# Expert 0 loaded before the router has run, the overflow branch behind the second pass, and two modulation vectors summed on VectorE

## The chip, the cores and the metric

The kernel runs as one program on one core of a Trainium2 chip. The metric is device time in microseconds (us) from one launch. The engines are TensorE (PE, with its weight loads as PEld), VectorE (DVE), ScalarE (ACT), GpSimd (POOL) and SyncE (SP), whose queue issues the loads of weights from HBM.

## The reference

`x` is 256 tokens of 1024 numbers. Two blocks follow one another, each of two layers. The first block is an even layer and an odd layer, and each layer has a token mixer and a mixture of 16 experts:

```python
mod = cond @ mod_w[layer] + mod_b[layer]            # six vectors of 1024 per layer
h = rms_norm(x, mix_norm_g[layer]) * (1 + sc1) + sh1
x = x + g1 * (even_mixer or odd_mixer)(h)
h = rms_norm(x, ffn_norm_g[layer]) * (1 + sc2) + sh2
x = x + g2 * moe(h)                                 # two of 16 experts per token
# moe, for the tokens of expert e:  (silu(xb @ w1[e]) * (xb @ w3[e])) @ w2[e]
# odd_mixer: proj = h @ od_in; conv of width 4; sigmoid gates; linear recurrence over
#            the tokens; gelu(y) * state; @ od_out
```

The second block has attention of three kinds and a dense MLP in each of its two layers, with six modulation vectors per layer for the tokens and for a context. All numbers are float32, and the six weights of an expert (two halves each of w1, w3 and w2) are 1 MB each, 96 MB per layer.

## The kernel before

The program goes through its stages once, in this order: even mixer and its output projection (to 181 us), router of layer 0 (to 217), experts of layer 0 (to 466), odd mixer and its output projection (to 582), router of layer 1 (to 620), experts of layer 1 (to 866), second block (to the end).

**Weights.** `weights` opens a pool for a stage with a ring of `raw` tiles: "long" has 11 tiles of 0.5 MB (the mixers), "wide" 9 tiles of 1 MB (router and experts), "short" 6 of 0.5 MB (second block). `load` (L321) takes the next tile and issues one DMA on SP's queue. That queue is in order: a load whose tile is still read holds up what stands behind it. In the mixers `linear` splits each weight into a high part on ScalarE (L332, `wh`) and a low part on VectorE (L325, `wl`) and multiplies three times on TensorE (L344 to L346). The experts' weights go to TensorE in float32 as they are (L959).

**Modulation vectors.** Each vector is a sum over eight loads of 0.5 MB. `mod_steps` makes eight units of it, which wait in a list and which `fill`, `need` and `settle` take off between other work. A unit is by default matmuls on TensorE into a bank of PSUM (L406); where `onv` holds an entry, VectorE multiplies and adds the load into tiles instead (L391 for the first load, L393 for the others), and TensorE only adds up the partitions at the end. Before, only vectors of the second block are summed on VectorE, with two conditions each.

**Experts.** `router` ranks the 16 experts by their number of tokens; `idi` holds the numbers in order of rank, and SP reads a register from it (L889) before it can address the weights. `PASSES` groups ranks: a pass of one rank has 128 columns of tokens, a pass of two has 64 per expert, and a pass of four 32 per expert, with the experts side by side in TensorE's array. `prep` gathers the tokens of a pass (L925 on VectorE, L933 to L944 on TensorE), `up_` multiplies by w1 and w3 (into `psab`), `down` by w2 (into `psY`), `combine` adds the results to `xT` (L1000). `sources` lists the loads in the order of use, and `taken` issues a load when its turn in the program comes and a tile is free. At the last pass but one (`p == NP - 2`) all engines come to a branch (L804): if an expert has more tokens than its columns, a loop serves the rest. With the inputs at hand the loop is not entered.

**Odd mixer.** Two loops over eight blocks of `od_in` (L1060 and L1062 apply the convolution on VectorE; L1087 copies the second half of the projection), with one modulation unit behind each block. Between the loops lie the gates and the recurrence: sigmoids, tanh, exponentials and logarithms on ScalarE (L293), two multiplications per block on GpSimd (L1072, L1081), a subtraction (L1079) and a scan (L1082) on VectorE.

A scheduler places the instructions of a stage on each engine within the order of the code; what stands where is read from the built programs below.

## Time and profile before

| | us |
|---|---|
| median of 3 runs (lowest, highest) | 1956.85 (1954.48, 1958.96) |
| the profiled execution | 1955.22 |
| its span in the trace | 1953.4 |
| experts of layer 0, 217 to 466 | 249 |
| odd mixer and output projection, 466 to 582 | 116 |
| experts of layer 1, 620 to 866 | 246 |
| second block, 866 to 1953.4 | 1087.4 |

The profile page has one line per 40 equal slices of the span (48.8 us each) for the engines, the granted clock of TensorE (PEclk) and the DMA engines, each digit a share in tenths; tables of busy time by window and by line; and lists of waits. A wait is named by who waited and who ended it.

### The profile page before, as it was taken

To read this page: it belongs to the slowest core of one execution; us is meant where nothing else is said; L and a number is where in the kernel's file an instruction comes from. 1 tells how busy PE (TensorE), PEld (TensorE's weight loads), DVE (VectorE), ACT (ScalarE), POOL (GpSimd) and SP (SyncE) were. 2 spreads that over 40 slices of the span, in tenths; PEclk is the share of its full clock that TensorE was granted. 3 is DMA by queue.
4 is the path that set the end of the run, shared out by engine and by line. 5 is a ranking of instruction groups with operands and counts; after the bars stand their busy time and mean duration, and the time that the engine had idled before them with its cause. 6 is when DMAs were issued, how large, how long until landed. Compare 5 with 4: busy or idle time off the path is not lost. (4 is left out here: it accounts for less than half of the span.)

```text
span 1953.4 us, 29087 instructions
## 1 busy us (share of the span) xinstructions
PE 1758.2 (90%) x11198; PEld 1256.4 (64%) x11198; DVE 1078.6 (55%) x2298; ACT 741.2 (38%) x1461; POOL 70.7 (4%) x88
## 2 busy tenths in 40 slices
PE   5999689967897799689999999999999999989997
PEld 4866234414783344237655779888888786669996
DVE  4987212104654112048778367678855767666665
ACT  3556100003642000124767355232323656544443
POOL 0000000000200000000010001000000200010000
PEclk8999899978998999889999999999999999989999
DMA  9685999997649999984100675555543220245551
GB/s 378 242 285 193 382 413 419 371 381 311 242 164 369 417 423 380 386 343 156 35 21 33 218 253 188 176 172 187 188 129 130 97 93 22 76 153 182 183 184 44
DMA packets 94361, 440.46 MB, mean 225 GB/s; under 512 B 10240, under 2 KB 10368, under 8 KB 69376
## 3 DMA queue, kind: packets, MB, share of 16 engines
q1 hardware_dynamic: 94208, 438.44, 60.0%
q8 instruction: 93, 1.52, 0.3%
q14 instruction: 60, 0.49, 0.1%
HBM read 437.35 MB, written 1.05 MB: 224 GB/s over the span
## 5 line engine op out<-in xcount | busy, mean ns | idle before, releaser
L332 ACT CAST wh<-raw 128x1024 fp32r<-128x1024 f32 (+1 forms) x258 | 261.4, 1016 | 281.8 <-PE psL L346 209.8
L325 DVE TENSOR_TENSOR wl<-raw,wh 128x1024 fp32r<-128x1024 f32 (+1 forms) x258 | 305.3, 1185 | 97.8 <-ACT wh L332 97.4
L959 PE MATMUL psab<-raw,xg 128*32 128x512 f32 (+2 forms) x1024 | 226.2, 705 | 76.1 <-DMA raw<-w 62.8
L344 PE MATMUL psL<-h,wh 128*128 128x256 f32 (+1 forms) x800 | 258.4, 323 | 7.6 <-ACT h L340 7.6
L345 PE MATMUL psL<-h,wl 128*128 128x256 f32 (+1 forms) x800 | 257.8, 323 | 4.0 <-DVE wl L325 3.9
L346 PE MATMUL psL<-h,wh 128*128 128x256 f32 (+1 forms) x800 | 256.4, 321 | 0.0
L959 PEld LDWEIGHTS psab<-raw,xg 128*32 128x32 f32 (+2 forms) x1024 | 73.9, 147 | 221.7 <-issue 193.7
L344 PE MATMUL psL<-gh,wh 128*128 128x256 f32 (+1 forms) x576 | 185.1, 322 | 0.0
L345 PE MATMUL psL<-gh,wl 128*128 128x256 f32 (+1 forms) x576 | 184.6, 321 | 0.0
L344 PEld LDWEIGHTS psL<-h,wh 128*128 128x128 f32 x800 | 154.2, 193 | 23.4 <-ACT h L340 8.3
L973 DVE SCALAR_TENSOR_TENSOR sa<-sa,gs,psab 128x512 f32<-128x512 f32 x14 | 10.5, 747 | 282.5 <-PE psab L959 282.5
L345 PEld LDWEIGHTS psL<-h,wl 128*128 128x128 f32 x800 | 154.2, 193 | 18.5 <-DVE wl L325 5.1
L346 PEld LDWEIGHTS psL<-h,wh 128*128 128x128 f32 x800 | 153.9, 193 | 14.2 <-issue 4.2
L959 PE MATMUL psY<-raw,at 128*32 128x512 f32 (+2 forms) x512 | 113.1, 611 | 9.3 <-DMA raw<-w 8.4
L346 PE MATMUL psL<-o,wh 128*128 128x256 f32 (+1 forms) x384 | 119.3, 311 | 0.3
L344 PEld LDWEIGHTS psL<-gh,wh 128*128 128x128 f32 x576 | 109.5, 190 | 14.5 <-issue 5.8
L345 PEld LDWEIGHTS psL<-gh,wl 128*128 128x128 f32 x576 | 109.5, 190 | 11.1 <-issue 3.7
L340 ACT CAST yh<-psY 128x512 fp32r<-128x512 f32 x28 | 16.4, 586 | 245.5 <-PE psY L959 245.5
L346 PE MATMUL psL<-gl,wh 128*128 128x256 f32 (+1 forms) x288 | 91.9, 319 | 0.0
L1525 ACT ACTIVATE t<-psL 128x256 f32<-128x256 f32 (+1 forms) x72 | 32.8, 456 | 139.1 <-PE psL L346 139.1
L1123 DVE SCALAR_TENSOR_TENSOR xT<-psL,mod2T,xT 128x256 f32<-128x256 f32 x80 | 38.6, 483 | 84.2 <-PE psL L346 84.0
L344 PE MATMUL psL<-hh,wh 128*128 128x256 f32 x256 | 77.8, 305 | 7.0 <-ACT hh L518 5.5
(449 smaller groups left out, 3340.9 us busy)
## 6 DMA issues: line engine op xcount, KB each, us to landing
raw<-w SPq DMA_DIRECT2D x192, 1024.0 KB, 11.7
raw<-fc SPq DMA_DIRECT2D x144, 512.0 KB, 3.5
raw<-mod_w SPq DMA_DIRECT2D x80, 512.0 KB, 6.6
raw<-w_mod SPq DMA_DIRECT2D x80, 512.0 KB, 3.9
raw<-wo SPq DMA_DIRECT2D x24, 512.0 KB, 4.7
raw<-wi SPq DMA_DIRECT2D x18, 512.0 KB, 3.3
raw<-ev_in SPq DMA_DIRECT2D x16, 512.0 KB, 7.4
raw<-mod_w SPq DMA_DIRECT2D x8, 1024.0 KB, 10.3
```

The lines of the kernel that those rows point to most:

```text
L325: eng.tensor_sub(o, a, hi)
L332: SC.copy(hi[:, :w], raw[:, :w])
L340: SC.copy(hi, src)
L344: T.matmul(o, lhsT=wh, rhs=xh, start=start, stop=False)
L345: T.matmul(o, lhsT=wl, rhs=xh, start=False, stop=False)
L346: T.matmul(o, lhsT=wh, rhs=xl, start=False, stop=stop)
L959: r = T.matmul(o[w * i:w * i + w, :], lhsT=x[:, w * i:w * i + w], rhs=loads[i][0][:, c:c + 512], start=first, stop=last)
L973: V.scalar_tensor_tensor(sa, sa, gs, ob, op0=OP.mult, op1=OP.mult)
L1123: V.scalar_tensor_tensor(src2[s][:, n, :], o[:, s * S:s * S + S], mod2T[l][:, g, s, n:n + 1], src2[s][:, n, :], op0=OP.mult, op1=OP.add)
L1525: SC.activation(t[:, a:b], o[:, a:b], AF.Relu)
```

## The change

Five things change together.

1. Expert 0, whatever its number of tokens, gets rank 0 (its sorting key is raised by 16·2S). Its weights can be addressed before the router has run. `PASSES` becomes `[[0], [8..11], [1], [2,3], [4,5], [12..15], [6,7]]`: rank 0 by itself first, the pass of four ranks second, a pass of two last.
2. The output projections become functions of their own (`even_out`, `out_proj`), and the ring of the experts is opened on the right side of SBUF before they begin. `hold` issues the six loads of expert 0 from within them. The nine tiles are now three `raw` and six `kept`; expert 0 fills the kept ones, and the later loads of the layer take turns through all nine. The long ring shrinks from 11 to 8 tiles, and the second block's ring moves to the right side.
3. The branch moves from the last pass but one to the place behind `up_` of the pass of four; the loop behind it has 32 rounds in place of 16.
4. In the odd mixer one vector is summed on TensorE at the start (`fill(8)`), and the two vectors of the two `od_in` loops are summed on VectorE, one condition each (`parts` is 1): two L391 and fourteen L393 instructions per vector. The eight units in the output projection are now a vector of the second block.
5. In the second block's first layer one vector is summed on TensorE before the first modulation (`fill(8, True)`); over the whole block one vector fewer is left for TensorE.

```diff
-PASSES = [[8, 9, 10, 11], [0], [2, 3], [4, 5], [1], [6, 7], [12, 13, 14, 15]]
-GROUPS = [[0, 1], [2, 3], [4, 5], [6]]
+PASSES = [[0], [8, 9, 10, 11], [1], [2, 3], [4, 5], [12, 13, 14, 15], [6, 7]]
+GROUPS = [[0], [1, 2], [3, 4], [5, 6]]
...
-        KINDS = {"long": (11, 1024, 4), "wide": (9, 2048, 0), "short": (6, 1024, 3)}
+        KINDS = {"long": (8, 1024, 4), "wide": (3, 2048, 0), "short": (6, 1024, 3)}
...
-            t = p.tile([128, cols], F32, tag="raw", bufs=n, name="raw")
+            t = p.tile([128, cols], F32, tag="kept" if held else "raw", bufs=6 if held else n, name="raw")
...
-                    for i in range(2):
+                    for i in range(parts):
                         for h in range(2):
                             a, w = acc[i][h], r[:, h * 512:h * 512 + 512]
...
+        def out_half(h, ch, cl, hold):
 
             for n in range(8):
+                if n in (3, 5, 7):
+                    hold()
...
-        def out_proj(src, ch, cl, l):
+        def out_proj(src, ch, cl, l, hold):
             need(("a", l, 2))
             for n in range(8):
+                if n > 1:
+                    hold()
...
+            V.tensor_scalar(key[:, 0:1], key[:, 0:1], 16.0 * 2 * S, None, op0=OP.add)
...
+        def holder(l, ring, held):
+
+            src = [A[w][l, 0, j] for w in ("w1", "w3", "w2") for j in range(2)]
+
+            def hold():
+                if len(held) < len(src):
+                    stream.append(ring)
+                    held.append((load(src[len(held)].rearrange("p a n -> p (a n)"), None, 2048, True), landing[0]))
+                    stream.pop()
+            return hold
...
-            known, ahead = {}, []
+            known, ahead, turns = {}, held, [0]
...
-                for p in range(NP + 1):
+                for p in range(1, NP + 1):
                     yield from up(p) if p < NP else ()
-                    yield from down(p - 1) if p else ()
+                    yield from down(p - 1) if p > 1 else ()
...
-                    ahead.append((load(w[l][expert(r), j].rearrange("o p a n -> p (o a n)"), None, 2048), landing[0]))
+                    ahead.append((load(w[l][expert(r), j].rearrange("o p a n -> p (o a n)"), None, 2048, turns[0] % 9 > 2),
+                                  landing[0]))
+                    turns[0] += 1
...
-            pr, at, todo, groups = prep(0), {}, [], list(range(1, len(GROUPS)))
-            for p in range(NP + 1):
+            pr, at, groups = prep(0), {}, list(range(2, len(GROUPS)))
+            first = up_(0, pr[0])
+            pr.update(prep(1))
+            todo = [(pr[0][1], down(0, first))]
+            for p in range(1, NP + 1):
                 if p < NP:
                     at[p] = up_(p, pr[p])
-                if p:
+                if p == 1:
+                    fetch(9)
+                    tables(sets[AF.Exp])
+                    overflow(l, th, tl, gt, slot, cap, mxc)
+                    new_block()
+                if p > 1:
                     todo.append((pr[p - 1][1], down(p - 1, at.pop(p - 1))))
...
-                if p == NP - 2:
-                    fetch(KINDS["wide"][0])
-                    tables(sets[AF.Exp])
-                    overflow(l, th, tl, gt, slot, cap, mxc)
-                    new_block()
...
-        def odd_mixer():
+        def odd_mixer(ch, cl):
+            fill(8)
+            onv.extend([1, 1])
...
+                fill(8, True)
+                onv.append(1)
```

On SP before, at the end of the even mixer's output projection and into the router (a row is a line of the code, an operation, the tile written and read, its shape and a count):

```order
L321 DMA raw<-mod_w 128x1024 x4
L321 DMA raw<-ev_out 128x512 x8
L321 DMA raw<-mod_w 128x2x1024 x8
L889 TENSOR_LOAD idi
L889 ISA x2
L321 ISA
L321 DMA raw<-w 128x2048
```

The same place of the changed program, where the first six `w` are expert 0's:

```order
L324 DMA raw<-mod_w 128x1024 x4
L324 DMA raw<-w 128x2048 x3
L324 DMA raw<-ev_out 128x512 x3
L324 DMA raw<-w 128x2048
L324 DMA raw<-ev_out 128x512 x2
L324 DMA raw<-w 128x2048
L324 DMA raw<-ev_out 128x512 x2
L324 DMA raw<-w 128x2048
L324 DMA raw<-ev_out 128x512
L324 DMA raw<-mod_w 128x2x1024 x8
L907 TENSOR_LOAD idi
```

Six loads of 1 MB moved ahead of the last eight loads of the projection and ahead of the eight loads of the router's modulation vectors; no register is read for them.

On TensorE before, from the end of the first `prep` (`psX`) into the experts (`psab` is the product with w1 and w3, 32x512 a pass of four ranks):

```order
L941 MATMUL psX<-cst_108,P 128x128 x2
L944 MATMUL psX<-rt,P 128x1 x2
L802 TENSOR_LOAD mxi
L802 ISA x2
L959 MATMUL psab<-raw,xg 32x512 x64
L959 MATMUL psab<-raw,xg 128x512 x2
L976 MATMUL psX<-cst_108,sa 128x128 x4
```

The same place in the changed program, and what follows its second `prep`:

```order
L961 MATMUL psX<-cst_121,P 128x128 x2
L964 MATMUL psX<-rt,P 128x1 x2
L979 MATMUL psab<-raw,xg 128x512 x16
L807 TENSOR_LOAD mxi
L807 ISA x2
L996 MATMUL psX<-cst_121,sa 128x128 x4
```

```order
L961 MATMUL psX<-cst_121,P 128x128 x2
L964 MATMUL psX<-rt,P 128x1 x2
L979 MATMUL psY<-raw,at 128x512 x8
L979 MATMUL psab<-raw,xg 32x512 x64
L996 MATMUL psX<-cst_121,sa 128x128 x4
L809 COMPARE_AND_BRANCH
```

Sixteen matmuls of expert 0 stand where the first pass of four stood; the second `prep`, expert 0's w2, the pass of four and then the branch follow.

On VectorE before, in the first `od_in` loop of the odd mixer (`wl` is the low part of a weight, `xc` the convolution):

```order
L325 TENSOR_TENSOR wl<-raw,wh 128x1024
L1060 TENSOR_SCALAR xc<-psL,pv 128x256
L325 TENSOR_TENSOR wl<-raw,wh 128x1024
L1062 SCALAR_TENSOR_TENSOR xc<-psL,pv,xc 128x255
L1060 TENSOR_SCALAR xc<-psL,pv 128x256
L1062 SCALAR_TENSOR_TENSOR xc<-psL,pv,xc 128x254
```

In the changed program (`acc` holds the sum of a modulation vector):

```order
L328 TENSOR_TENSOR wl<-raw,wh 128x1024
L395 TENSOR_SCALAR acc<-raw,cond_88 128x512 x2
L328 TENSOR_TENSOR wl<-raw,wh 128x1024
L1085 TENSOR_SCALAR xc<-psL,pv 128x256
L397 SCALAR_TENSOR_TENSOR acc<-raw,cond_88,acc 128x512
L1087 SCALAR_TENSOR_TENSOR xc<-psL,pv,xc 128x255
L397 SCALAR_TENSOR_TENSOR acc<-raw,cond_88,acc 128x512
```

Two sums of 512 columns per block now stand among the splits and the convolution, sixteen in this loop and sixteen more from its end into the recurrence.

## Rows read from the trace of the kernel before

**Rows 1.** The page: span, and DMA share in tenths of 40 slices.
```profile
span 1953.4 us, 29087 instructions
...
DMA  9685999997649999984100675555543220245551
```
**Rows 2.** Windows at layer 0's router: busy us, counts, PEclk, DMA share, GB/s.
```profile
170.00:181.00 11.00, 10.70 (x88) 10.29 (x86) 7.74 (x15) 7.13 (x13) 0.00 (x0) 1.00 0.31 97
181.00:202.00 21.00, 16.40 (x179) 8.14 (x179) 15.08 (x53) 9.72 (x24) 1.59 (x2) 1.00 0.90 351
```
**Rows 3.** Windows in the experts of layer 0.
```profile
217.00:244.80 27.80, 15.23 (x96) 3.77 (x96) 0.00 (x0) 0.60 (x1) 0.00 (x0) 0.82 1.01 426
...
372.00:390.00 18.00, 18.00 (x84) 7.11 (x84) 1.76 (x4) 1.55 (x3) 0.00 (x0) 1.00 0.72 281
390.00:414.00 24.00, 14.05 (x74) 4.30 (x72) 1.38 (x2) 4.53 (x6) 0.00 (x0) 0.78 0.82 333
...
457.50:466.00 8.50, 7.96 (x42) 3.32 (x42) 3.15 (x7) 3.04 (x5) 0.00 (x0) 0.80 0.06 17
```
**Rows 4.** Waits of TensorE from 217 to 466: total us, times, longest.
```profile
PE psab L959 <- DMA raw<-w: 32.5, 9, 6.4
```
**Rows 5.** TensorE in order of time: start, us, count, [idle before <-releaser].
```profile
210.04 1.93 PE L406 MATMUL psab<-raw,cond1r 128*32 128x256 f32 x32
...
217.00 3.64 PE L959 MATMUL psab<-raw,xg 128*32 128x512 f32 x32 [1.98 <-DMA raw<-w]
...
253.66 0.48 PE L933 MATMUL psX<-P,th 128*128 128x256 f32 x2
...
258.78 1.53 PE L959 MATMUL psab<-raw,xg 128*128 128x512 f32 x3
...
340.59 14.00 PE L959 MATMUL psab<-raw,xg 128*128 128x512 f32 x32
...
401.14 9.80 PE L959 MATMUL psab<-raw,xg 128*32 128x512 f32 x64 [6.89 <-DVEq L804]
```
**Rows 6.** SP in order of time: the runs of expert loads of both layers.
```profile
202.73 58.37 SPq L321 DMA_DIRECT2D raw<-w  x26
...
606.10 93.72 SPq L321 DMA_DIRECT2D raw<-w  x43
```
**Rows 7.** DMA issues from 202.5 to 203: KB, us from issue to landing.
```profile
raw<-w SPq DMA_DIRECT2D x1, 1024.0 KB, 4.7
```
**Rows 8.** Windows in the experts of layer 1.
```profile
778.00:790.00 12.00, 12.00 (x55) 4.10 (x52) 0.75 (x1) 0.60 (x1) 0.00 (x0) 1.00 0.86 340
...
815.00:858.30 43.30, 31.93 (x170) 11.20 (x170) 6.04 (x12) 1.17 (x2) 0.00 (x0) 0.84 1.01 426
```
**Rows 9.** Windows in the odd mixer (PE, PEld, DVE, ACT, POOL).
```profile
475.50:509.00 33.50, 30.90 (x257) 28.20 (x258) 30.42 (x56) 13.43 (x18) 0.00 (x0) 0.86 0.87 335
509.00:522.00 13.00, 13.00 (x85) 12.16 (x85) 1.91 (x4) 12.95 (x30) 5.86 (x8) 1.00 0.58 215
522.00:538.00 16.00, 10.54 (x97) 7.09 (x97) 12.33 (x20) 14.00 (x35) 6.81 (x8) 0.74 0.63 211
538.00:552.00 14.00, 14.00 (x112) 14.00 (x112) 13.14 (x23) 9.93 (x20) 0.00 (x0) 0.94 0.79 289
...
566.00:582.00 16.00, 14.85 (x142) 13.17 (x134) 3.67 (x9) 2.02 (x3) 0.00 (x0) 1.00 0.07 9
```
**Rows 10.** VectorE by line and shape over the span: busy us, mean ns.
```profile
L393 DVE SCALAR_TENSOR_TENSOR sq<-raw,cond,sq 128x512 f32<-128x512 f32 x112 | 77.3, 744 | 1.2 <-DMA raw<-w_mod 1.2
...
L391 DVE TENSOR_SCALAR sq<-raw,cond 128x512 f32<-128x512 f32 x16 | 7.2, 479 | 5.1 <-PE psM L397 5.1
```
**Rows 11.** GpSimd in order of time, end of the recurrence.
```profile
533.73 0.73 POOL L1081 TENSOR_TENSOR ix<-ix,uu 128x256 f32<-128x256 f32 x1 [0.87 <-ACT uu L293]
535.33 1.72 POOL L1081 TENSOR_TENSOR ix<-ix,uu 128x256 f32<-128x256 f32 x1 [0.87 <-ACT uu L293]
```
**Rows 12.** VectorE in order of time, the same place.
```profile
535.26 1.19 DVE L325 TENSOR_TENSOR wl<-raw,wh 128x1024 fp32r<-128x1024 f32 x1
```
**Rows 13.** Window of the second block.
```profile
866.00:1953.40 1087.40, 1044.10 (x6516) 838.51 (x6516) 746.97 (x1460) 512.55 (x1018) 54.61 (x64) 0.99 0.40 133
```

More of the change, by code (lines that the diff above doesn't have):

```diff
@@ L1579, in body, with block @@
[L1579 to L1589 removed]
+            def block():
+                return Act(8, S, F32R, "cath"), Act(8, S, F32R, "catl")
@@ new lines, in body @@
+            SY.dma_start(out=cT, in_=A["cT"])
+            with ExitStack() as right:
+                with weights("od", "long"), phase("odk"):
+                    banks.clear(); banks.update(L=3, X=2, M=1, G=2)
+                    (ch, cl), held = block(), []
+                    with phase("od", False):
+                        odd_mixer(ch, cl)
+                        settle()
+                    ring = right.enter_context(weights("moe1", "wide", "right", False))
+                    out_proj(A["od_out"], ch, cl, 1, holder(1, ring, held))
+                    settle()
+                stream.append(ring)
+                with phase("moe1"):
+                    banks.clear(); banks.update(ab=3, Y=2, X=3)
+                    moe(1, held)
+                stream.pop()
```

128 lines of the change are left out of this document (63 added, 65 removed).

## The prediction

> **What bounds the kernel now.** I read the slices first [rows 1]: the DMA engines are full in four stretches and nearly idle in others, so no one engine bounds the whole. The windows then tell the stages apart. The experts of each layer are bound by DMA: behind 217 us TensorE is busy for 15.23 of 27.8 us while 426 GB/s arrive [rows 3], and its longest waits there are for expert weights, 32.5 us in all [rows 4]. At 426 to 429 GB/s a load of 1 MB (1.049 million bytes) takes 2.44 us. The 96 loads of layer 0 begin to move at about 205.0 (first issue 202.73, landing 4.7 later, less 2.44) [rows 6, 7] and end at 457.5, where the DMA share falls to 0.06 [rows 3]. That is 252.5 us for 96 x 2.44 = 234.2, so 18.3 us are lost; the largest holes lie at 372 to 390 (share 0.72, 5 us) and 390 to 414 (0.82, 4.3 us) [rows 3], behind the single-rank pass and at the branch. In layer 1 the loads begin 403.4 us later (606.10 against 202.73 [rows 6]) and end at 858.3 [rows 8], so 15.7 us are lost. Ahead of both routers DMA idles: share 0.31 from 170 to 181 [rows 2], 0.07 from 566 to 582 [rows 9]. The odd mixer is bound by VectorE in its first loop (30.42 busy of 33.5 us), then by ScalarE (12.95 of 13.0 and 14.0 of 16), then by TensorE [rows 9]. The second block is TensorE (1044.10 of 1087.4 [rows 13]).
>
> **Expert 0 ahead of the router.** Twelve loads leave the bound stages: 6 x 2.44 = 14.7 us of DMA per layer. They go into idle DMA time, and cost the projection little in layer 0: at a share of 0.31, some 7.6 us are free in the 11 us to 181, and as much again in the 10 us ahead. But the ring still has nine tiles, and six of them hold expert 0 until TensorE has used it. So I follow the ring.
>
> TensorE ends the first `prep` now at 215.0 (217.00 less its wait of 1.98 [rows 5]). With one rank to prepare instead of two passes I take 213.5. Three loads of the pass of four find free tiles and have landed by then or soon after (215.7). The next six need a tile of expert 0. One rank by itself takes 14.00 us for four loads, 3.5 us each [rows 5], so tiles come free at 217.0, 220.5, 224.0 and 227.5; the second `prep` takes 258.78 - 253.66 = 5.1 us and the transposes 0.6; the two loads of w2 are used at 236.7 and 240.2. Each new load lands 4.7 us later, the last at 244.9. DMA has then moved nine loads, 22.0 us of work, in 39.9 us: 17.9 us idle, where before it ran at a share of 1.01 all this time [rows 3]. **The preload is nearly eaten by its own ring.** Next comes the pass of four. Its first batch (3.64 us) frees four tiles at 243.8, landing 248.5, 1.2 us late. Behind it stands rank 1 by itself, 3.5 us a load against 2.44: with every tile full this costs 1.06 us on each of four loads, 4.3 us. From about 300 on TensorE has, by the durations of such passes, some 125 us of work left and DMA 145, and no pass holds nine tiles for long: nothing more is lost. The branch, 6.89 us of waiting on TensorE now [rows 5], finds nine loads (22 us) on their way and costs DMA nothing.
>
> Sum for layer 0: 205.0 + 90 x 2.44 + 17.9 + 1.2 + 4.3 = 448.0 against 457.5, 9.5 us gained; with two ranks instead of four in the last batch I add 0.5: **-10**. So the gain is the holes of before that go, not the 14.7 us. Layer 1, the same ring 403.4 us later: 851.4 against 858.3, **-7**, since it has fewer holes to lose. The bounds: each us by which expert 0 begins earlier or later moves the end by as much, and the start lies between 208 (P is ready, no modulation matmuls of 1.93 us [rows 5] in the way) and 217: -15 to -6 and -12 to -3.
>
> **The odd mixer pays.** Each vector on VectorE is 2 x 0.479 + 14 x 0.744 = 11.4 us [rows 10]. The first one's operations stand between the splits and the convolutions of the first loop, where VectorE has 33.5 - 30.42 = 3.1 us to spare [rows 9]. TensorE loses two times 1.93 us there, which doesn't help, since it isn't last. 30.4 + 11.4 = 41.8 busy, at the same fine stalls 43: +9.5 (8.3 to 11.4). Everything behind waits for the last convolution: the gates on ScalarE, the recurrence, the rest of the projection. The second vector finds VectorE idle for 11.1 of the 13 us after the loop [rows 9]; ten of its accumulations stand there, four (3.0 us) among the subtractions and scans, on the path: +2 (0 to 5). TensorE has about two us less of modulation matmuls when it becomes last again (538 to 552, 14.00 of 14.00 [rows 9]); I take -1. Together **+10.5** (6 to 16). The vector on TensorE at the start runs while the norm keeps VectorE and ScalarE busy, and is hidden; if it isn't, it costs 3.9.
>
> GpSimd's last multiplication takes 1.72 us instead of 0.73 where VectorE runs a split with two inputs in SBUF [rows 11, 12]; a multiplication and such an operation don't run side by side there. The Trainium skill ("SBUF — State Buffer", section "SBUF: two separate sides") says so: the two engines share a pair of ports under an exclusive lock, also where a VectorE operation has two SBUF inputs and the GpSimd one reads SBUF. The trace agrees (1.72 against 0.73 us). By it the four accumulations beside the recurrence would hold GpSimd for 0.74 us each, 3 us more than I take, and the odd mixer would stand at +13.5.
>
> **The rest.** The long ring of 8 delays some weights of the even mixer's heads, which stand on SP behind modulation loads waiting for a tile; who waits is TensorE. There is no row for it; the nearest is the stretch from 170 to 181, where DMA at 0.31 keeps TensorE at 10.70 of 11 busy [rows 2]: 0 to +4, I take +1.5. In the odd projection two of the eight loads of `od_out` stand behind five or six MB of expert 0 (14.6 us), needed some 20 us after its start: 0 to +5, I take +1. The modulation loads behind them on SP come early or on time. The second block has one vector fewer on TensorE, 2 x 1.93 = 3.9 us, and one moved to its beginning, part of which meets idle time: -4 to +1, I take **-3**. The longer loop behind the branch is not entered: 0. One more VectorE operation in the router: +0.2.
>
> **Sum**: -10 - 7 + 10.5 + 1.5 + 1 - 3 + 0.2 = -6.8. The profiled execution took 1955.22 us (span 1953.4); it lies 1.6 below the median of the runs, 1956.85. So 1948.4 for such an execution, and 1950.0 for the median.
>
> **Rivals.**
> *The ring dries less.* Expert 0 begins at 208, since the modulation matmuls have been done before. Then all six tiles come free 5.5 us earlier in both layers: -11, 1939.0. For it: the router's modulation loads are partly fetched earlier, in time that is idle now [rows 2]. Against it: six of those eight loads go through three tiles and each waits for matmuls, and DMA carries 351 GB/s there already [rows 2].
> *It doesn't do what it says.* Expert 0 waits for SBUF of the mixer stage, lands late and delays the router's modulation vectors; the gain of the experts halves (8.5 instead of 17), with the rest as above: 1958.5, or 1954 if the odd mixer comes out at its lower end. It shows as expert 0's loads behind 181 us.
> *Slower: VectorE's bill in full.* In the odd mixer the second vector is on the path as well, since ScalarE and VectorE take turns in the recurrence and each accumulation comes between: 22.8 instead of 10.5 us. 1950.0 + 12.3 = 1962.3. It decides from +21.2 in the odd mixer on (10.5 + 6.8 + 3.9). For it: the recurrence is a chain of four engines, busy 12.33 of 16 us on VectorE already [rows 9]. Against it: ten of fourteen accumulations stand ahead of the first subtraction.
>
> **How the numbers follow.** A change under 0.2% (3.9 us) can't be told from none here. Forecast 0.50, the dry ring's rival 0.15, the one without gain 0.15, VectorE's bill 0.20. The forecast's terms give about +-7 around 1950.0; of its 0.50 some 0.35 lie below 1952.9, 0.12 within 0.2%, 0.03 above 1960.8. The first rival is faster; the second is 0.02 faster, 0.09 the same, 0.04 slower; the third is 0.02 the same, 0.18 slower. Faster 0.52, same 0.23, slower 0.25. The range takes in the forecast, the first rival but for its end, and VectorE's bill at its price: 1936 to 1963; its two sides leave out about 0.2.
>
> **What would show it.** In the profile after: expert 0's six loads landed before the router (right), a hole of about 18 us in the DMA slices while expert 0 runs (right, and the main point; if it is under 10, the ring was misread); expert loads that end near 448 and, counted from the router, as far on in layer 1; VectorE over 0.95 busy in the first `od_in` loop and that loop 9 to 10 us longer. Wrong would be: TensorE waiting in the output projections, an even mixer more than 4 us longer, or an odd mixer that keeps its 116 us.

## The result, and the profile after

The changed kernel takes 2002.09 us (median of 4 runs, 1999.71 to 2009.69) where the kernel before, on the same chip, takes 1957.9 (4 runs, 1954.48 to 1959.37): a ratio of 1.0235, with a 95% interval of 1.0203 to 1.0267. It is 2.3% slower. The forecast was 0.35% faster, and the time lies outside the range. The profiled execution after took 2000.16 us, its span is 1998.3; 44.9 us more than the span of before are to be found. In the kernel after, line numbers are higher than before (splits on L328 and L335, the products on L347 to L349, experts on L979).

The page of after, its span and its DMA slices (50 us each), which answer to [rows 1]:

```profile
span 1998.3 us, 28869 instructions
...
DMA  8667798999776789997310265545543331055551
```

The two slices ahead of the routers, the fourth and the twelfth, are 7 now, where they were 5 and 4 in [rows 1]. The idle DMA time was filled, as the change meant to, and yet the end is later. A table by stage, from the start and end of each stage's matmuls and vector operations in the two traces, says where:

| stage | before | after | difference |
|---|---|---|---|
| start to the last matmul of the even attention | 157.6 | 164.3 | +6.7 |
| output projection, even layer | 23.7 | 30.3 | +6.6 |
| router of layer 0, to `idi` | 20.4 | 22.8 | +2.4 |
| experts of layer 0, `idi` to the last combine | 264.1 | 265.4 | +1.3 |
| odd mixer, to the last scan | 72.0 | 86.1 | +14.1 |
| output projection, odd layer | 40.7 | 45.3 | +4.6 |
| router of layer 1 | 26.8 | 27.9 | +1.1 |
| experts of layer 1 | 259.6 | 262.7 | +3.1 |
| second block | 1088.5 | 1093.5 | +5.0 |

A single stage is known to a few us only. The even mixer with a ring of 8 ends between 159.9 and 164.3 in the kernel after and six below, with a ring of 11 between 157.0 and 157.7. The expert stages last 260 to 265 us in kernels that leave them as before; in the four kernels that have the expert code of after (after itself and three below) they last 265.4 to 272.2 us in layer 0 and 262.7 to 265.1 in layer 1, so the kernel after stands at their low end in both.

**The projections.** Windows of the kernel before (even projection, then the second `od_in` loop's end and the odd projection) and of after (the same two), with busy us and counts of PE, PEld, DVE, ACT and POOL, PEclk, DMA share, GB/s:

```profile
157.60:181.30 23.70, 22.97 (x194) 21.09 (x192) 18.65 (x42) 17.21 (x34) 0.00 (x0) 1.00 0.32 99
538.00:578.50 40.50, 40.50 (x354) 39.13 (x357) 25.32 (x43) 16.20 (x28) 0.00 (x0) 0.98 0.44 151
```

```profile
164.30:194.60 30.30, 24.62 (x203) 21.74 (x201) 16.55 (x35) 15.67 (x31) 0.00 (x0) 1.00 0.95 385
569.00:615.00 46.00, 41.27 (x351) 37.92 (x350) 22.64 (x40) 14.31 (x25) 0.00 (x0) 0.96 0.88 334
```

Before, TensorE is busy 22.97 of 23.7 and 40.50 of 40.5 us while DMA runs at 0.32 and 0.44: the projections are bound by TensorE. After, DMA runs at 0.95 and 0.88, and TensorE stands still for 5.7 and 4.7 us. The waits of ScalarE, which splits the weights, for loads of the projection, in the even and in the odd projection of after (total us, times, longest):

```profile
ACT wh L335 <- DMA raw<-ev_out: 4.8, 3, 2.5
...
ACT wh L335 <- DMA raw<-od_out: 18.5, 2, 14.6
```

**The experts.** TensorE of after in order of time, which answers to [rows 5] (start, us, count, [idle before <-releaser]); rank 0 with w1 and w3, its w2, the pass of four in three batches, the second prep behind the branch, rank 1:

```profile
228.27 13.98 PE L979 MATMUL psab<-raw,xg 128*128 128x512 f32 x32
...
248.70 7.11 PE L979 MATMUL psY<-raw,at 128*128 128x512 f32 x16
255.74 7.07 PE L979 MATMUL psab<-raw,xg 128*32 128x512 f32 x64
269.96 5.47 PE L979 MATMUL psab<-raw,xg 128*32 128x512 f32 x32 [7.15 <-DMA raw<-w]
280.51 5.32 PE L979 MATMUL psab<-raw,xg 128*32 128x512 f32 x32 [5.08 <-DMA raw<-w]
...
294.23 0.77 PE L953 MATMUL psX<-P,th 128*128 128x256 f32 x2 [6.72 <-DVEq L809]
...
300.82 13.98 PE L979 MATMUL psab<-raw,xg 128*128 128x512 f32 x32
```

and the windows of the same time, which answer to [rows 3]:

```profile
228.00:261.00 33.00, 32.09 (x153) 16.43 (x155) 7.89 (x32) 5.76 (x10) 0.00 (x0) 1.00 0.69 237
261.00:300.00 39.00, 19.03 (x125) 9.39 (x117) 2.82 (x4) 2.84 (x5) 0.00 (x0) 0.78 1.00 415
300.00:330.00 30.00, 29.89 (x152) 14.04 (x153) 6.68 (x16) 4.17 (x7) 0.00 (x0) 1.00 0.76 289
330.00:475.40 145.40, 116.53 (x594) 45.52 (x592) 19.66 (x38) 8.97 (x16) 0.00 (x0) 0.91 1.01 419
```

While rank 0 holds its six tiles, DMA runs at 0.69 where it ran at 1.01 before [rows 3]; then TensorE starves (19.03 busy of 39 us); then rank 1 by itself frees tiles more slowly than DMA fills them (0.76). The last load lands 258.0 us behind `idi`, 255.8 before: the six loads bought nothing.

**The odd mixer.** Windows of before, first loop to the last convolution and from there to the last scan; then the same two of after (they answer to [rows 9]):

```profile
475.60:507.50 31.90, 29.30 (x236) 27.32 (x240) 28.85 (x53) 13.20 (x17) 0.00 (x0) 0.85 0.87 336
507.50:537.80 30.30, 24.84 (x206) 19.84 (x196) 15.51 (x28) 26.87 (x63) 12.67 (x16) 0.86 0.63 217
```

```profile
491.50:534.90 43.40, 34.06 (x257) 29.72 (x250) 38.85 (x71) 15.96 (x22) 0.00 (x0) 0.91 0.81 279
534.90:568.90 34.00, 21.63 (x135) 18.77 (x135) 31.70 (x46) 28.23 (x65) 18.03 (x16) 0.80 0.63 206
```

VectorE has 10.0 us more to do in the first loop, which is 11.5 longer, and 16.2 more behind it, which is 3.7 longer. GpSimd's same sixteen operations cost 5.4 us more there.

**The second block.** The waits of TensorE in its first 45 us (900 to 945; in the 45 us from 860 before, the longest is 2.7):

```profile
PE psO L422 <- ACT k L419: 4.9, 1, 4.9
PE psO L411 <- DMA raw<-w_mod: 4.3, 4, 1.6
```

They belong to the vector that is now summed at the start of the block.

### The profile page after: what moved, and what is told of

Same layout as the page of the kernel before. It is cut to its first block, busy times and chain, and to the rows that moved or that the text cites. A ratio compares the mean times of both kernels' runs of the same rounds, so it can differ in the third digit from the quotient of the medians.

```text
span 1998.3 us, 28869 instructions
## 1 busy us (share of the span) xinstructions
PE 1772.3 (89%) x11086; PEld 1257.9 (63%) x11086; DVE 1103.5 (55%) x2332; ACT 740.8 (37%) x1461; POOL 71.5 (4%) x88
## 4 chain that ended last, share of the span: by engine, by line
PE 52%; DMA 5%; DVE 4%; ACT 2%; issue 1%; POOL 0%; SPq 0%; ACTq 0%; DVEq 0%; POOLq 0%
PE psL L347 11%; PE psL L349 11%; PE psL L348 11%; DMA raw<-w 4%; PE psO L1307 2%; PE psab L979 2%; PE psY L979 2%; PE psT L1300 2%; PE psS L1497 2%; PE psS L347 1%; DVE wl L328 1%; DMA raw<-w_mod 1%; PE psS L348 1%; PE psS L349 1%; PE psX L1180 1%
## 5 line engine op out<-in xcount | busy, mean ns | idle before, releaser
L335 ACT CAST wh<-raw 128x1024 fp32r<-128x1024 f32 (+1 forms) x258 | 261.4, 1016 | 315.8 <-PE psL L349 208.0
L328 DVE TENSOR_TENSOR wl<-raw,wh 128x1024 fp32r<-128x1024 f32 (+1 forms) x258 | 307.6, 1194 | 101.0 <-ACT wh L335 100.3
L979 PE MATMUL psab<-raw,xg 128*32 128x512 f32 (+2 forms) x1024 | 224.2, 701 | 64.9 <-DMA raw<-w 64.8
L347 PE MATMUL psL<-h,wh 128*128 128x256 f32 (+1 forms) x800 | 256.9, 321 | 7.6 <-ACT h L343 7.6
L348 PE MATMUL psL<-h,wl 128*128 128x256 f32 (+1 forms) x800 | 258.0, 323 | 4.4 <-DVE wl L328 4.3
L349 PE MATMUL psL<-h,wh 128*128 128x256 f32 (+1 forms) x800 | 256.1, 321 | 0.0
L979 PEld LDWEIGHTS psab<-raw,xg 128*32 128x32 f32 (+2 forms) x1024 | 73.9, 146 | 206.4 <-issue 179.8
L347 PE MATMUL psL<-gh,wh 128*128 128x256 f32 (+1 forms) x576 | 184.8, 321 | 0.0
L347 PEld LDWEIGHTS psL<-h,wh 128*128 128x128 f32 x800 | 152.5, 191 | 23.8 <-ACT h L343 8.3
L993 DVE SCALAR_TENSOR_TENSOR sa<-sa,gs,psab 128x512 f32<-128x512 f32 x14 | 10.5, 748 | 274.3 <-PE psab L979 249.5
L349 PEld LDWEIGHTS psL<-h,wh 128*128 128x128 f32 x800 | 151.9, 190 | 15.7 <-issue 4.6
L979 PE MATMUL psY<-raw,at 128*32 128x512 f32 (+2 forms) x512 | 113.4, 637 | 10.9 <-DMA raw<-w 10.8
L349 PE MATMUL psL<-o,wh 128*128 128x256 f32 (+1 forms) x384 | 119.7, 312 | 0.6
L347 PEld LDWEIGHTS psL<-gh,wh 128*128 128x128 f32 x576 | 108.3, 188 | 15.7 <-issue 5.8
L348 PEld LDWEIGHTS psL<-gh,wl 128*128 128x128 f32 x576 | 108.3, 188 | 12.4 <-issue 3.7
L349 PE MATMUL psL<-gl,wh 128*128 128x256 f32 (+1 forms) x288 | 92.0, 319 | 0.0
L979 PEld LDWEIGHTS psY<-raw,at 128*32 128x32 f32 (+2 forms) x512 | 36.3, 136 | 76.1 <-issue 64.0
L347 PE MATMUL psL<-hh,wh 128*128 128x256 f32 x256 | 78.0, 305 | 6.5 <-ACT wh L335 3.8
```

The lines of the kernel that those rows point to most:

```text
L328: eng.tensor_sub(o, a, hi)
L335: SC.copy(hi[:, :w], raw[:, :w])
L347: T.matmul(o, lhsT=wh, rhs=xh, start=start, stop=False)
L348: T.matmul(o, lhsT=wl, rhs=xh, start=False, stop=False)
L349: T.matmul(o, lhsT=wh, rhs=xl, start=False, stop=stop)
L979: r = T.matmul(o[w * i:w * i + w, :], lhsT=x[:, w * i:w * i + w], rhs=loads[i][0][:, c:c + 512], start=first, stop=last)
```

## The experiments

Where a run has one time, it stands beside before on the same chip; then the stages carry the verdict, not the total, since 19 runs of before on one chip lie between 1952.0 and 1968.1 us. A stretch of 17 us at a granted clock of 0.50 (1.2 GHz) falls at varying places of the second block in some runs and costs some 8 us (an estimate, half its length); where it counts, it is named.

### The ring of eight alone

```diff
# the kernel before
-        KINDS = {"long": (11, 1024, 4), ...
+        KINDS = {"long": (8, 1024, 4), ...
```

> The kernel before with the mixers' ring of 8 tiles instead of 11, nothing else. Theory A (the shorter ring alone delays the weights of the heads in the even mixer, which stand on SP's queue behind loads of modulation vectors that wait for a tile): the last attention matmul moves from 157.6 us to about 164 (it ends at 164.3 in the changed kernel), the odd mixer grows by 0 to 3 us, the total by 6 to 10. Rival (the even mixer is longer because of the split of its stage in two pools, or of the order that the scheduler found): no more than 2 us.

Measured: 1974.48 us against 1956.44, more than either theory allowed. The attention ends 4.1 us later, the even projection is 2.7 longer (its granted clock is 0.94, before 1.00, so part of that may be chance), the odd projection 8.9 (49.6 against 40.7), and the router behind it 2.2; the second block's share is within the scatter. SP's queue shows it. It is in order, and its loads of weights and of modulation vectors alternate. The first load of `od_out`, in the kernel before and with the ring of eight (start, us):

```profile
526.49 0.38 SPq L321 DMA_DIRECT2D raw<-od_out  x1
```

```profile
544.08 0.33 SPq L321 DMA_DIRECT2D raw<-od_out  x1
```

The last scan ends 5.1 us later with the ring of eight (542.9 against 537.8), the first load of the projection comes 17.6 later: with three tiles fewer the queue stands in the recurrence, where no one frees a tile, and the loads ahead don't suffice. ScalarE's waits in the following projection:

```profile
ACT mod_e L414 <- PE psM L406: 14.1, 2, 11.4
ACT wh L332 <- PE psL L346: 12.6, 4, 5.8
ACT wh L332 <- DMA raw<-od_out: 7.2, 2, 4.3
```

The even projection has the same: its last eight loads of `ev_out` begin at 166.18, before at 143.79. The prediction's +1.5 for the ring was far too small, and it looked at the even mixer alone.

### Two vectors on VectorE alone

```diff
# the kernel before; the odd mixer's ring is 10 tiles, the sums need the room
         def odd_mixer():
+            fill(8)
+            onv.extend([1, 1])
...
-                    for i in range(2):
+                    for i in range(parts):
```

> The kernel before with one vector on TensorE at the start of the odd mixer and the two vectors of its loops on VectorE; its ring has 10 tiles for want of space. Theory A (VectorE bounds the first loop and stands in the recurrence): from the first hl to the last convolution 42 to 44 us instead of 31.9, the end of the scans 13 to 15 us later, the second block 3 to 5 us shorter, the total 7 to 12 us longer. Rival (the longer odd mixer of the changed kernel comes from its ring of 8 and from the DMA of expert 0): the odd mixer grows by less than 5 us and the total by nothing.

Measured: 1966.11 against 1956.44. From the end of the experts to the last scan 87.6 us (72.0 before), the odd projection 37.5 (40.7), the second block 1085.6 (1088.5). The first loop:

```profile
472.30:516.00 43.70, 33.60 (x237) 30.04 (x229) 38.02 (x69) 15.04 (x21) 0.00 (x0) 0.88 0.81 272
```

It is the loop of the kernel after (43.40 us, VectorE 38.85), without the other edits (the ring has 10 tiles here, 8 there). So the odd mixer's bill is VectorE's, as forecast, and the second block's gain of 2.9 for a vector less on TensorE is there too, as long as nothing is moved to its start.

### The kernel after without those vectors

```diff
# the kernel after
         def odd_mixer(ch, cl):
-            fill(8)
-            onv.extend([1, 1])
```

> The changed kernel with the odd mixer's vectors back on TensorE (no vector at its start, none on VectorE). Theory A (the vectors on VectorE cost the odd mixer 12 to 15 us by themselves): from the first hl to the end of the scans 62 to 66 us instead of 77.4 (62.2 before), one vector more for TensorE in the second block (+3 to +4), the total 7 to 12 us below the changed kernel. Rival (the odd mixer is long because its ring has 8 tiles): 73 us or more, total within 4 us of the changed kernel.

Measured: 2010.51 against 1959.97. The mixer gives back what was expected (first operation to last scan 65.0 us, after 77.4, before 62.2), but the total does not fall: the odd projection is 56.2 us instead of 45.3, and the second block has a vector more and several short stretches of low clock (1102.1). ScalarE in the odd projection:

```profile
ACT wh L335 <- DMA raw<-od_out: 18.4, 2, 15.6
ACT mod_e L419 <- PE psM L411: 11.1, 2, 8.3
ACT wh L335 <- PE psL L349: 9.8, 4, 4.3
```

The two edits are tied. With a ring of eight and expert 0 in the queue, modulation units on TensorE cost the stage about as much as VectorE's sums do: the mixer is 12.4 us shorter and the projection 10.9 longer.

### Expert 0 loaded behind the projections' own loads

```diff
# the kernel after: no hold() in the two projections
-        def moe(l, held):
+        def moe(l, held, hold):
...
+            for _ in range(6):
+                hold()
```

> The changed kernel with the six loads of expert 0 issued behind the router's modulation loads instead of inside the output projections. Theory A (the loads crowd the projection's own weights, and the nine tiles dry up while expert 0 runs, so that loading early buys nothing): even projection back from 30.3 to 24 us, the hole of DMA while expert 0 runs under 8 us instead of 17, experts from the router's idi to their end 250 to 258 us instead of 265.4, the total 15 to 25 us below the changed kernel. Rival (loading early does buy time, which something else eats): experts 10 to 15 us longer, the total within 5 us or longer than the changed kernel.

Measured: 1999.5 against 1956.44, of which some 8 us are a stretch of low clock at 1676. The even projection is 24.9 us (after 30.3), the odd one 38.1 (45.3). In the built program three of the six loads stand between the router's vectors; SP in layer 0:

```profile
175.77 0.38 SPq L324 DMA_DIRECT2D raw<-ev_out  x1
176.20 0.43 SPq L324 DMA_DIRECT2D raw<-mod_w  x1
176.68 1.58 SPq L324 DMA_DIRECT2D raw<-w  x3
189.97 14.95 SPq L324 DMA_DIRECT2D raw<-mod_w  x5
204.98 1.74 SPq L324 DMA_DIRECT2D raw<-w  x3
```

All six stand behind the last load of the projection, but three still land before `idi` (by 192.2, `idi` is at 209.1), and in layer 1 four do. So this run moves expert 0 in the queue; it isn't a kernel without loading ahead. From `idi` the experts take 270.6 and 265.5 us, not less than after, as theory A had it. The holes between the landings from 226 to 260 us still add up to 16 us (theory A: under 8), and at layer 0 TensorE waits for the pass of four as it does in the kernel after:

```profile
265.31 5.75 PE L977 MATMUL psab<-raw,xg 128*32 128x512 f32 x32 [7.00 <-DMA raw<-w]
275.85 5.34 PE L977 MATMUL psab<-raw,xg 128*32 128x512 f32 x32 [4.79 <-DMA raw<-w]
```

So putting the six loads ahead of the projections' own costs these 5.4 and 7.2 us. What it is worth to the experts is less clear: against the kernel after it would be 5.2 and 2.8 us, but the four kernels with all six tiles loaded there take 265.4 to 272.2 and 262.7 to 265.1 us, so that in layer 0 no gain is shown, and in layer 1 at most 3 us. The rival's 10 to 15 us didn't come either.

### Four tiles held instead of six

```diff
# the kernel after: w1 and w3 of expert 0 ahead, its w2 in its turn
-        KINDS = {"long": (8, 1024, 4), "wide": (3, 2048, 0), "short": (6, 1024, 3)}
+        KINDS = {"long": (8, 1024, 4), "wide": (5, 2048, 0), "short": (6, 1024, 3)}
...
-            t = p.tile([128, cols], F32, tag="kept" if held else "raw", bufs=6 if held else n, name="raw")
+            t = p.tile([128, cols], F32, tag="kept" if held else "raw", bufs=4 if held else n, name="raw")
...
-            src = [A[w][l, 0, j] for w in ("w1", "w3", "w2") for j in range(2)]
+            src = [A[w][l, 0, j] for w in ("w1", "w3") for j in range(2)]
...
+                yield from [(A["w2"], 0, 0), (A["w2"], 0, 1)]
...
```

> The changed kernel with four kept tiles instead of six and five for the rest: w1 and w3 of expert 0 are loaded ahead, w2 in its turn behind the router; nine tiles as before. Theory A (what is loaded ahead only moves the hole, since the nine tiles are what limits): two loads fewer ahead cost 4.9 us of DMA, and two tiles more for the next pass give as much back, so the experts take 262 to 267 us from the router's idi to their end as now (265.4), less 2 to 4 us since the router's modulation loads have five tiles; the even projection 2 us shorter. Rival (loading ahead counts for itself): experts 4 to 6 us longer.

Measured: 1999.19 against 1961.0. The even projection is 2.6 us shorter (27.7), the experts 3.9 and 6.0 longer from `idi`; the first lies within the four kernels with six tiles, the second (268.8) above them. The hole in front of the pass of four is 7.6 us, as with six. The odd projection is 4.5 shorter (40.8). The two projections and the two expert stages together take 603.7 us in the kernel after, and 607.2 and 609.5 in the two kernels below that differ from it in the second block alone; with four tiles they take 606.5, with the six loads behind the projections' own (the run before this one) 599.1, and in the kernel before 588.1. So four tiles instead of six can't be told from six: what the projections gain, the experts lose. The place in the queue is worth 5 to 10 us, and none of these versions comes near the kernel before.

### The order of the passes alone

```diff
# the kernel before: no loading ahead, nine equal tiles
-PASSES = [[8, 9, 10, 11], [0], [2, 3], [4, 5], [1], [6, 7], [12, 13, 14, 15]]
+PASSES = [[0], [8, 9, 10, 11], [1], [2, 3], [4, 5], [12, 13, 14, 15], [6, 7]]
# and the branch behind up_ of the pass of four
```

> The kernel before with the new order of passes and the branch behind the first pass of four, without any early load; expert 0 is not forced to be the first. Theory A (a rank by itself, 3.5 us a load, dries the ring wherever TensorE is behind with all nine tiles full, and the order decides little): experts of layer 0 between 247 and 256 us from 217 on instead of 249, total within 8 us of before. Rival (the new order removes the holes at 383.9 and 412.2 and gains by itself): experts 8 to 11 us shorter per layer, the total 15 to 20 us below before.

Measured: 1962.74 against 1956.44; the experts last 264.3 and 262.5 us from `idi`, as before (264.1, 259.6), with the last load at 456.7 (457.5). Short stretches of low clock in the second block (at 1126 and 1160) account for part of the rest. TensorE around the branch and rank 1, and the window of rank 1:

```profile
277.75 0.77 PE L935 MATMUL psX<-P,th 128*128 128x256 f32 x2 [6.24 <-DVEq L804]
...
285.09 13.98 PE L961 MATMUL psab<-raw,xg 128*128 128x512 f32 x32
```

```profile
286.00:310.00 24.00, 24.00 (x106) 9.15 (x105) 1.81 (x4) 2.21 (x4) 0.00 (x0) 1.00 0.74 264
```

The DMA share of 0.74 with TensorE at 24.00 of 24 us is the hole of the kernel after at its rank 1 (0.76), without any loading ahead. The branch and the prep behind it keep TensorE from freeing tiles, the ring fills up, and then a rank by itself opens it at 3.5 us a load. Landings show some 10 us lost there, 5.1 of it at once; the prediction counted 4.3.

### Another order of passes

```diff
# the kernel before
+PASSES = [[8, 9, 10, 11], [0], [12, 13, 14, 15], [1], [2, 3], [4, 5], [6, 7]]
```

> The kernel before with another order of its passes: the second pass of four ranks third, rank 1 by itself fourth, the pairs last; no early load, branch still at the last pass but one. Theory A (a rank by itself opens a hole in the DMA stream, 3.5 us a load against 2.44, only where TensorE is behind and all nine tiles are full; behind a pass of four TensorE waits for loads and has slack): the hole of 7.1 us at rank 1 in layer 0 and of 4.5 us in layer 1 shrinks below 3 us, the experts are 4 to 8 us shorter per layer, the total 1942 to 1950 us. Rival (the hole belongs to rank 1 wherever it stands, or goes to the next pass): total within 4 us of before.

Measured: a ratio of 0.9994 (0.9981 to 1.0006), the same. The largest hole falls from 7.1 to 2.1 us, as the theory had it, but the total is the rival's. The last load lands at 455.0 instead of 457.5, which is no more than scatter: from `idi` that is 253.9 us, and kernels that leave the experts alone show 253.1 to 256.3. The tail behind the last load grows from 8.3 to 12.4 us: a pair of ranks ends the stage instead of a batch of four.

### The second block without the vector at its start

```diff
# the kernel after
-                fill(8, True)
-                onv.append(1)
...
             if l == 0:
+                onv.append(1)
                 ka = chunk(2, 512)
```

> The changed kernel without the vector on TensorE at the beginning of the second block; that block then has one vector more for TensorE later. Theory A (eight loads and their matmuls stand ahead of the first weights there, on SP and on TensorE, where the weights of the projection would else arrive): from the end of the experts of layer 1 to the first rope matmul back from 27.6 to 23 us, and to the third rope stage 8 to 10 us earlier; the MLP gives 4 us back, so the total falls by 4 to 6 us. Rival (TensorE is idle there and the vector is free): no gain at the start, total 3 to 4 us longer.

Measured: 1996.78 against 1959.97. The experts' end to the first rope takes 22.8 us (27.6 after, 22.8 before), the second block 1088.8 (1093.5). The longest wait of TensorE from 900 to 945 is again

```profile
PE psS L347 <- ACT h L343: 2.7, 1, 2.7
```

as before. The vector at the start meets no idle time; it costs 4.7 us more there than later in the block.

### The side of SBUF of the second block's weights

The change also moves the second block's ring to the right side of SBUF. The prediction gave this no term. Two runs move that ring alone:

```diff
# the kernel before, then the kernel after
-            st.enter_context(weights("b2", "short"))
+            st.enter_context(weights("b2", "short", "right"))
...
-            st.enter_context(weights("b2", "short", "right"))
+            st.enter_context(weights("b2", "short"))
```

> The kernel before with the second block's ring of weights on the right side of SBUF, nothing else. In the changed kernel the matmuls of 512 columns in the second block start every 233.3 ns instead of 227.0 and those of 256 columns every 116.7 instead of 119.7. Theory A (the place of the tiles in SBUF does it): the same two figures here, the first MLP 5 us longer, the second 4 to 5 us shorter, the total within 4 us of before. Rival (that run had another TensorE clock or other inputs of its matmuls): 227.0 and 119.7 as before.

> The changed kernel with the second block's ring on the left side again. Theory A (side of SBUF): 227.0 and 119.7 ns between matmul starts, total within 4 us of the changed kernel. Rival: 233.3 and 116.7 ns.

Measured: 1972.51 and 1997.23 us, both against 1959.97. The first has 17 us at a clock of 0.50 at 1649. Windows of 50 us in the two MLPs (512 columns a matmul in the first, 256 in the second), all at a granted clock of 1.00. In the kernel before (left), and in the kernel before with the ring on the right:

```profile
1280.00:1330.00 50.00, 50.00 (x234) 40.64 (x233) 39.96 (x63) 13.76 (x18) 0.00 (x0) 1.00 0.54 175
1780.00:1830.00 50.00, 49.93 (x416) 49.73 (x415) 31.70 (x43) 23.12 (x34) 0.00 (x0) 1.00 0.55 180
```

```profile
1280.00:1330.00 50.00, 50.00 (x228) 39.51 (x227) 38.89 (x60) 15.94 (x22) 0.00 (x0) 1.00 0.51 169
1800.00:1850.00 50.00, 49.88 (x423) 49.67 (x423) 31.94 (x44) 23.54 (x34) 0.00 (x0) 1.00 0.53 184
```

In the kernel after (right), and in the kernel after with the ring on the left:

```profile
1300.00:1350.00 50.00, 50.00 (x229) 39.53 (x228) 31.47 (x47) 17.95 (x26) 0.00 (x0) 1.00 0.44 136
1820.00:1870.00 50.00, 49.85 (x427) 49.65 (x426) 32.81 (x44) 23.43 (x34) 0.00 (x0) 1.00 0.59 189
```

```profile
1300.00:1350.00 50.00, 50.00 (x234) 40.60 (x234) 34.14 (x51) 18.03 (x26) 0.00 (x0) 1.00 0.42 138
1820.00:1870.00 50.00, 49.93 (x416) 49.73 (x416) 31.47 (x43) 22.89 (x34) 0.00 (x0) 1.00 0.55 184
```

TensorE is full in all eight. On the left it does 234 matmuls in the first window and 416 in the second, on the right 228 or 229 and 423 or 427. By the starts of neighbouring matmuls, 512 columns take 227 ns on the left and 233 on the right, 256 columns 119.6 to 120.0 and 116.7 to 117.5. In the kernel before the first MLP is 6.6 us longer with the ring on the right (323.9 against 317.3); in the kernel after, the second block is 3.8 us shorter with it on the left.

Two more runs tried to have the faster side in each layer: the whole ring opened per layer, or only the two parts `wh` and `wl`, left in layer 0 and right in layer 1. (The expectations call these parts 16-bit halves; the profile has them as fp32r tiles.)

```diff
# the kernel before: the whole ring per layer
+                with weights(f"b2{l}", "short", "right" if l else None):
...
# the kernel before: raw tiles as they were, the halves per layer
-            q, b = stream[-1][0], stream[-1][4]
+            q, b = halves[0] or stream[-1][0], stream[-1][4]
...
+                    halves[0] = sl.enter_context(tc.tile_pool(name=f"w_{l}", bufs=1, side="right" if l else None, reuse_waits=RW))
```

> The kernel before with the second block's pool of weights opened per layer: on the left side for the first layer, on the right for the second; the tiles of the activations lie below it in both. In the earlier runs the left side gave 227.0 ns between matmuls of 512 columns (first layer) and 119.7 to 120.0 of 256 (second layer), the right side 233.3 and 116.8 to 117.5. Theory A (the side of the weights decides): 227 and 117, the second layer 5 to 6 us shorter, the total 1949 to 1953 us. Rival (the place of the activations decides, which lie here in both layers where they lie with the right side): 233 and 117, the first layer 5 us longer, no gain.

> The kernel before, with one change in the second block: the raw tiles of the weights stay where they were for both layers, and the two 16-bit halves of each load stand in a pool of their own for each layer, on the left side of SBUF for its layer 0 and on the right side for its layer 1. Theory A (the place of the 16-bit halves in SBUF sets the rate of the matmuls, 119.7 against 116.8 ns at 256 columns, 227 against 233 at 512): rates of 227 ns in layer 0 and 117 ns in layer 1, layer 1 about 6 us shorter than before, and the passage between the layers not longer than before by more than 2 us, since the raw tiles wait for nothing new; 1949 to 1957 us, a ratio of 0.994 to 0.998. Rival: the halves of layer 1 stand where tiles of layer 0 stood and wait for them, as with the whole pool per layer, so that the passage takes 8 us more: a ratio of 1.000 to 1.004.

Measured: ratios of 1.0033 (1.0015 to 1.0052) and 1.004 (1.0025 to 1.0055). The rates are those of the weights' side (the second MLP's window has x424 and x425), with the activations where they stood before. But at the change of layers TensorE now waits for the first split weight of layer 1. The second run's rival had foreseen this, since the tiles of layer 1 lie where tiles of layer 0's MLP lay; the profile shows the wait, not the places. The whole ring per layer first:

```profile
PE psS L344 <- ACT wh L332: 15.2, 1, 15.2
```

```profile
PE psS L344 <- ACT wh L332: 13.5, 1, 13.5
```

No such wait is there before (the first rope comes 22.9 us after the last norm of layer 0; 32 and 30 here). So in the first run theory A was right on the rates and wrong on the total, and its rival (the activations' place) was wrong on the rates; in the second run the rival was right, with a ratio in its range. No version here beats the kernel before.

## Why the prediction was wrong

Two steps failed. Behind the first nine new loads the prediction let the experts lose almost nothing more, and they lost 17.1 us in layer 0 instead of 5.5. And it took the output projections for nearly free, since DMA had idle time there; that their own loads stand behind expert 0's in the queue it priced for two loads alone, at 1 us, and they became 11.2 us longer. Two of its own three signs of being wrong came: TensorE waits in the output projections, and the even mixer is over 4 us longer.

**The experts' gain** (forecast -17, measured +4.4 by `idi`). In layer 0 the ring was read rightly up to the ninth new load: forecast 43.2 us behind `idi` (244.9 less 201.7), measured 43.3 (260.7 less 217.4). From there 81 loads of 2.44 us are 197.6; the forecast added 5.5 of holes, the trace shows 214.7, so 17.1. Three things are in the 11.6 that were missed:

1. Rank 1's hole is 8.8 us, not 4.3. The failed step is "the branch ... finds nine loads (22 us) on their way and costs DMA nothing". TensorE runs no expert matmul from 285.83 to 300.82. The last load on its way lands at 303.21, rank 1 frees its first tile at 304.5, and the next load lands at 309.43. The order of the passes alone shows the same hole.
2. Holes of about 1 us each, 4.2 together, against 1.2 forecast.
3. Loads that follow each other without a hole land 2.49 us apart, not 2.44: some 4 us over 81 loads, or 419 GB/s over the last 145 us instead of 426. This belongs to the changed ring: all six kernels that have it show a median of 2.49 us in both layers, the other eight 2.44 to 2.45, also on the same chip. The order of the passes alone has the old rate:

```profile
330.00:400.00 70.00, 53.23 (x305) 23.72 (x307) 10.05 (x21) 5.43 (x10) 0.00 (x0) 0.92 1.01 427
```

Whether the right side of SBUF or the split into `raw` and `kept` tiles does it was not tested.

So in layer 0 the forecast gain of 9.5 us became a loss of some 2, by the landing of the last load. Layer 1 has the same rate and holes of the same size (10.3 and 6.3 us between two landings at their largest, 10.2 and 6.2 in layer 0); its sum was not taken apart. The step "no pass holds nine tiles for long: nothing more is lost" was argued from sums of work (125 us against 145) where a queue had to be followed load by load, as had been done for expert 0.

**The projections** (forecast +1, measured +11.2). "They go into idle DMA time" is true and was not the question. The projection's own loads stand on the same in-order queue, behind expert 0's: ScalarE waits 18.5 us for `od_out`. With expert 0 behind them the two projections are 5.4 and 7.2 us shorter. In the even layer the prediction gave this no term at all; in the odd one it priced two of eight loads, and took a value near the lower end of its own 0 to 5.

**The long ring** (forecast +1.5 in 0 to 4, by itself +18.0). The row taken as nearest, TensorE at 10.70 of 11 us [rows 2], was of a stretch where the ring had been filled well ahead; how far ahead is what the ring's size decides. In the even mixer the forecast lies under what every kernel with a ring of eight shows (2.3 to 6.7 us). The ring's cost in the odd projection was not thought of. It is not paid in the kernel after, though: with the vectors on VectorE its first load of `od_out` is issued 18.7 us ahead of the last scan, before 11.3, and with expert 0 out of the way the odd projection takes 38.1 us with a ring of eight (37.5 with ten, on the kernel before).

**The odd mixer** (forecast +10.5, of it -1 behind the last scan; measured +14.1 to the last scan). Right in kind: the first loop +11.5 (forecast 9.5), the part behind it +3.7 (2), the stretch ahead of it -1.1. VectorE was 0.90 busy in the loop, not over 0.95. The kernel before with these vectors alone shows the same. The Trainium skill ("SBUF — State Buffer", section "SBUF: two separate sides") states that VectorE and GpSimd share a pair of ports under an exclusive lock. The trace agrees: GpSimd's two lines take 1257 and 1030 ns in the kernel after and 733 and 856 before,

```profile
L1097 POOL TENSOR_TENSOR ix<-ix,xc 128x256 f32<-128x256 f32 x8 | 9.8, 1257 | 333.1 <-DVE xc L1087 332.9 <-ACT ix L293 0.2
L1106 POOL TENSOR_TENSOR ix<-ix,uu 128x256 f32<-128x256 f32 x8 | 8.2, 1030 | 12.4 <-ACT uu L293 12.4
```

and without the two vectors, in the kernel after but for them, fourteen of these sixteen operations take 0.72 to 0.74 us again; with them three do. The prediction had priced this at 3 us and the odd mixer then at +13.5, which is nearer. In part that is luck: behind the first loop it would give 5 us where 3.7 were measured, and the first loop was 2 us longer than forecast. The rival of VectorE's bill in full (22.8) did not come.

**The second block** (forecast -3, measured +5.0). One vector less on TensorE is worth 2.9, as forecast; the vector moved to its start costs 4.7 and hides nothing; the other side of SBUF, for which the prediction had no term, costs 3.8. The three give +5.6.

The sum of the misses: experts 21.4, projections 10.2 with the ring's part, even mixer 5.2, odd mixer 3.6, second block 8.0, routers 3.3. That is 51.7, the distance from -6.8 to +44.9. No single rival stood for it, since each moved one term; what was common to them, that a ring of fewer tiles and a fuller queue make every stage around it wait, was priced at 2.5 us and is worth some 22 by this account (6.7 in the even mixer, 11.2 in the projections, 4.5 at rank 1).

What stays open: what of the even mixer's 6.7 us is the ring and what is scatter (kernels with this ring give 2.3 to 6.7); why layer 0's experts differ by 7 us between kernels with the same code there; what in the changed ring slows the loads from 2.44 to 2.49 us; and whether a ring of more than nine tiles for the experts would turn the balance, which wasn't tried.

## What to carry to other kernels

Idle DMA time ahead of a bound stage is worth only as much as the tiles in which the early loads wait, and the early loads belong behind the loads of the stage that is still running. If the tiles come from the ring of the stage before or of the stage itself, the time is moved, not won, so follow the in-order queue load by load through the first full drain and through each point where the consumer stops (a branch, a prep), and through the stage that lends the tiles. When a ring is made smaller, look for the longest time in which no tile is freed in each stage that uses it; the loads that were issued ahead of that time are what the stage behind lives on.

## What the runs showed of the hardware

The place of the stationary weights in SBUF changes TensorE's rate, at the same granted clock of 1.00: with the weights' tiles on the left side a matmul of 512 columns starts every 227 ns and one of 256 every 119.6 to 120.0, on the right every 233 and every 116.7 to 117.5. It follows the weights and not the activations, since the runs that moved the weights per layer show the left rate in layer 0 and the right rate in layer 1. Matmuls of 512 columns (measured in layer 0's MLP) are faster from the left, those of 256 (layer 1's MLP) from the right, and over this block the two nearly cancel. What in the place decides was not separated from the side.

Loads of 1 MB that follow each other without a hole land 2.44 to 2.45 us apart in the eight kernels with the old ring of the experts and 2.49 us apart in the six with the changed one (right side of SBUF, nine tiles split into `raw` and `kept`). Which of the two differences decides is open.
